# Spacing the loads, combinations and splits of the weight operands in the first layer of a two-layer encoder kernel

## The chip, the cores and the metric

The kernel runs on one core of a Trainium2 chip. The metric is the device time of one execution in microseconds (us). Three timed runs before the change took 2755.72, 2760.79 and 2751.14 us, so the median is 2755.72. A further execution was taken with the hardware profiler; all profile lines below are from it.

## The reference

Two layers over 2048 frames of width 1024, in float32. The change touches the first one, a chunked gMLP:

```
h = rms_norm(x, a_norm_g)
u, v, z = split(h @ w_in, 3)                  # w_in: 1024 x 6144
u = gelu(u);  v = layer_norm(gelu(v), ln_g, ln_b)
mixed = W_s(masked, per head) @ v in groups of 128 frames + b_s
x = x + (u * mixed * silu(z)) @ w_out         # w_out: 2048 x 1024
```

The second layer computes shared keys and values, a banded attention with a relative bias, a gate and an output product, and a last RMS norm ends the program. The second layer's code is not touched.

## The kernel before

**Numbers in two parts.** Each float32 operand of a product is split into a high part `hi` (an ACT cast to fp32r, L250) and a low part `lo` (source minus `hi`, on DVE, L253). `mm3` (L95) does hi x hi, hi x lo and lo x hi (L96, L97, L98), 128x128 against 128x512 each.

**Seven products for eight.** The input projection is made in six passes n = 0 to 5 (0 and 1 the two halves of v, 2 to 5 a quarter of u beside a quarter of z each), and the product with `w_out` in an output pass "o". Each multiplies a 2x2 block matrix by a 2x2 block matrix with seven block products, the phases 1 to 7, in the order `PH = (1, 2, 6, 5, 7, 4, 3)` (L439). The left operand of a phase is a block or a sum of blocks of the frames, `S`. The right one is a block or a combination of blocks of the weights, `T`. A phase has eight steps j, one for each pair of 128-frame blocks. A step of the input pass takes 4 x 3 matmuls into one PSUM tile `P`; passes 0 and 1 share their steps in phases 1 and 2, so those steps have twice as many. A step of the output pass takes 8 x 3 (tile `Po`). `evict` (L351) then brings the tile to SBUF: in phase 1 by an ACT copy (L357), else by a DVE sum with an earlier phase's tile (L353).

**Left operands.** In pass 0 they are made from normed frames by transposes and `s_split` (L390), and stored to memory (`hsd`, L397). Later passes load them with `s_load` (L383, DMA at L385) into six buffers `S`, asked for three steps ahead (`LOOK = 3`). In the output pass `prep_out` (L748) loads gated tiles (`A<-ytd`, four buffers), adds or subtracts them (phase 5 on DVE, L758; phase 7 on POOL, L762) and splits them (`So`).

**Right operands.** `make_t` (L258) has two functions for each piece q (two pieces in the input pass, four in the output one). `combine` loads 128x1024 pieces of weights, 512 KB each, into four buffers with the tag `raw` (L267; the profile's `rw`, `rwo`), and adds or subtracts them on POOL in halves of 512 columns (L272). Phase 6 takes three loads a piece and leaves a chain tile `ch` that phases 5 and 4 go on with; phase 7 takes two loads a piece, phases 1, 2, 3 and 4 one. `finish` splits the result into `T` (eight buffers; some phases use `hh` and `hl` instead).

**When things are listed.** `run_steps` (L442) goes from step -3 on. In each step it lists the events of the step, the product and eviction, the left operand of three steps later, and then what `add_t` (L458) has entered for that step. `add_t` computes `s = min(at + i, max(at, -1))`: where `at` is not negative, all pieces of a phase, loads, combinations and splits, come in the one step `at`, five steps before the phase starts. Phase 6 of passes 1 to 5 has its `combine` eight steps earlier still. The list is not yet the order on the engines. A planner goes through it with its own estimates of durations and may put an instruction whose inputs and buffers it holds ready earlier on its engine; each engine, and SP's queue that issues all DMAs, then runs its instructions strictly in the order so made. `behind` (L237) adds an edge for the planner between two instructions, with no semaphore; `in_order` uses it for the splits of left operands, and `merge_u` (L595) lists itself behind `last["evict"]`, the last DVE sum of an eviction.

**Around the products.** In passes 2 to 5, `uz_consts` (L543) loads `lg`, `lb` and the mixing weights `wr`, clears a corner on POOL (L554) and splits them to `ws`, all in one step, eight before the pass. `mix_prep` (L559) loads `va` (L564), applies the layer norm in two DVE instructions for each half (L568, L569) and splits to `vh`, `vl`, all in one step, four before the mixing products `mx` of `mix` (L577), which ACT evicts (L591). `done_uz` (L608) gates a finished tile through `later`, one to four steps after its eviction; `transposes` (L599) turns it on PE, ACT copies it out (L604) and it is stored to `ytd`. `flush` (L409) lists what has come due. After the last input step, `flush(1 << 30)` (L728) lists all that is left at once, ahead of the output pass. `block_norm` (L475) norms the frames at the start: ACT sums squares (L482), DVE adds EPS (L483), POOL takes the power (L484), DVE multiplies (L485).

Of the kernel before, what the change touches and what calls it, by code (L numbers as in the profile page):

```python
# [17 lines left out]
P = 128  # L18
# [15 lines left out]
def trunk_kernel(  # L34
# [174 lines left out]
    with ExitStack() as actx:  # L209
# [38 lines left out]

        def split(hi, lo, src, key=None):
            ins = nc.scalar.copy(hi, src)  # L250
            if key:
                in_order(key, ins)
            nc.vector.tensor_tensor(lo, src, hi.bitcast(F32), op=sub)  # L253
# [4 lines left out]
        def make_t(n, ph, src, nq, where, chain_of):  # L258
# [3 lines left out]
            vs = [None] * nq  # L262

            def combine(q):
                def raw(r, c):
                    t = sh.tile([P, 1024], F32, tag="raw", name=f"rw{n}_{ph}_{r}{c}{q}", bufs=4)
                    nc.sync.dma_start(t[:], src[r, c, q])  # L267
                    return t[:]

                def comb(o, x_, y_, op=sub):  # L270
                    for c in (slice(0, 512), slice(512, 1024)):
                        nc.gpsimd.tensor_tensor(o[:, c], x_[:, c], y_[:, c], op=op)  # L272
                    return o

                if ph in (1, 2, 3):
                    v = raw(*((0, 0), (1, 0), (1, 1))[ph - 1])
# [6 lines left out]
                elif n == "o":  # L283
                    if ph == 6:
                        if q == 0:
                            chain[n] = chain_of()
                        b = raw(1, 1)
                        v = comb(chain[n](q), b, raw(0, 1))
                        comb(v, v, raw(0, 0), add)
                    else:  # L290
                        v = raw(1, 1)
                        comb(v, v, chain[n](q))
                elif ph == 6:
                    if q == 0:
                        chain[n] = chain_of()
                    b = raw(0, 1)
                    t1 = comb(chain[n](2 + q), b, raw(0, 0))
                    v = comb(chain[n](q), raw(1, 1), t1)
                else:
                    v = chain[n](2 + q)  # L300
# [6 lines left out]
            return out, [  # L307
                [lambda q=q, f_=f_: f_(q) for q in range(nq)] for f_ in (combine, finish)
            ]

# [991 lines left out]
```

## Time and profile before

| | |
|---|---|
| median of 3 runs | 2755.72 us (2751.14 to 2760.79) |
| the profiled execution's own time | 2755.94 us |
| its span, first to last instruction | 2754.2 us |
| mean granted TensorE clock | 0.988 |
| input passes | to about 1086 us |
| output pass | about 1086 to 1425 us |
| DMA | 607.16 MB, mean 220 GB/s |
| PE idle before it, for S<-hsd | 15.6 us in 3 waits |

How to read the lines in the prediction. In a table of stretches, the columns are the stretch, its length, the busy time and number of instructions of PE, PEld (weight load), DVE, ACT and POOL, then the granted TensorE clock as a share of full speed, the DMA engines' mean busy share and GB/s. A timeline row has the start, the duration, the engine, the line, the operation, what it writes and reads, and in brackets the idle time of the engine before it and what ended that. SPq is the queue that issues the DMAs; the duration of a merged row there includes the waits between. A row of waits has the total us, the number and the longest. A row of a group has the busy time, the mean ns of one, and the idle time before them; a row of a tile or line gives min/median/max in ns and the first and last start in us. A DMA row has the size and the median us from issue to landing.

### The profile page before, as it was taken

How to read it: one execution, taken by the hardware profiler on the slowest of the kernel's cores; microseconds unless marked ns; L12 is line 12 of the kernel's file. 1: busy time of each engine (PE TensorE's matmuls, PEld its weight loads, DVE VectorE, ACT ScalarE, POOL GpSimd, SP SyncE). 2: the span in 40 equal slices, each digit the busy share in tenths (PEclk: the TensorE clock that was granted, in tenths of full speed). 3: DMA queues.
4: the chain of work that ended last, by engine and by line, in shares of the span. 5: the costliest groups of instructions: out<-in, count | busy, mean ns of one | idle time of the engine just before them, and what ended most of it. 6: DMA issues, size and time to landing. Idle time of an engine off the chain costs nothing.

```text
span 2754.2 us, 39945 instructions
## 1 busy us (share of the span) xinstructions
PE 2670.3 (97%) x14176; PEld 2269.1 (82%) x14176; DVE 1938.7 (70%) x3211; ACT 1274.9 (46%) x2244; POOL 717.1 (26%) x775
## 2 busy tenths in 40 slices
PE   8998989999999999998999999999999999999997
PEld 7787777888888877876888888899988999889996
DVE  5654556767567567676767676877778777887777
ACT  5422233443433424332235555566655666556663
POOL 4511124241231412536014531221112111121111
PEclk9999999999999999999999999999999999999998
DMA  8898997786877868767867665455554555453332
GB/s 288 318 322 295 334 341 281 262 309 231 312 266 241 307 204 287 278 228 252 295 198 235 223 196 190 154 153 154 157 167 159 154 152 151 145 169 112 121 111 69
DMA packets 209190, 607.16 MB, mean 220 GB/s; under 512 B 24288, under 2 KB 24288, under 8 KB 208992
## 3 DMA queue, kind: packets, MB, share of 16 engines
q1 hardware_dynamic: 208992, 604.62, 65.9%
q8 instruction: 113, 1.85, 0.3%
q14 instruction: 85, 0.70, 0.1%
HBM read 466.11 MB, written 127.93 MB: 216 GB/s over the span
## 4 chain that ended last, share of the span: by engine, by line
PE 44%; DVE 7%; DMA 5%; POOL 2%; issue 1%; ACT 1%; SPq 0%; DVEq 0%; POOLq 0%; ACTq 0%
PE pj L96 5%; PE pj L97 5%; PE pj L98 5%; PE s L973 4%; PE tp L1012 4%; PE pv L1039 4%; PE vp L96 2%; PE vp L98 2%; PE vp L97 2%; PE bo L96 2%; PE bo L97 2%; PE bo L98 2%; DMA rwo<-in_w_out 1%; DMA xr<-in_x 1%; DMA A<-ytd 1%
## 5 line engine op out<-in xcount | busy, mean ns | idle before, releaser
L96 PE MATMUL P<-T,S 128*128 128x512 f32 x1280 | 511.6, 400 | 18.2 <-DMA S<-hsd 15.6
L98 PE MATMUL P<-T,S 128*128 128x512 f32 x1280 | 504.0, 394 | 0.0
L97 PE MATMUL P<-T,S 128*128 128x512 f32 x1280 | 503.1, 393 | 0.5 <-DVE T L253 0.5
L992 POOL TENSOR_SCALAR pr<-pr,sl 128x640 f32<-128x640 f32 (+4 forms) x256 | 200.1, 782 | 759.5 <-DVE sl L991 669.7
L988 ACT ACTIVATE pr<-pr,nm 128x640 f32<-128x640 f32 (+4 forms) x256 | 195.5, 764 | 272.3 <-DVE nm L981 270.3
L96 PE MATMUL pj<-hh_b,wh_b 128*128 128x512 f32 x768 | 312.0, 406 | 0.7 <-ACT hh_b L150 0.7
L97 PE MATMUL pj<-hl_b,wh_b 128*128 128x512 f32 x768 | 302.7, 394 | 0.0
L98 PE MATMUL pj<-hh_b,wl_b 128*128 128x512 f32 x768 | 301.5, 393 | 0.0
L96 PEld LDWEIGHTS P<-T,S 128*128 128x128 f32 x1280 | 242.5, 189 | 63.7 <-DMA S<-hsd 14.0
L98 PEld LDWEIGHTS P<-T,S 128*128 128x128 f32 x1280 | 242.2, 189 | 51.7
L97 PEld LDWEIGHTS P<-T,S 128*128 128x128 f32 x1280 | 243.0, 190 | 44.9 <-DVE T L253 1.0
L1016 DVE TENSOR_TENSOR pt<-tp,pt 128x640 fp32r<-128x640 f32 (+4 forms) x256 | 188.6, 737 | 59.6 <-ACT pt L1015 57.0
L981 DVE CUSTOM_DVE_ANT_0 pr<-s,bias 128x640 f32<-128x640 f32 (+4 forms) x256 | 188.0, 735 | 44.5 <-PE s L973 41.1
L98 PEld LDWEIGHTS pj<-hh_b,wl_b 128*128 128x128 f32 x768 | 144.5, 188 | 33.3
L1015 ACT CAST pt<-tp 128x640 fp32r<-128x640 f32 (+4 forms) x256 | 159.3, 622 | 21.5 <-PE tp L1012 16.2
L1012 PE MATMUL tp<-ident,pr 128*128 128x128 f32 x1120 | 164.6, 272 | 4.4 <-DVE pt L1016 4.1
L96 PEld LDWEIGHTS pj<-hh_b,wh_b 128*128 128x128 f32 x768 | 144.9, 189 | 19.7 <-ACT hh_b L150 0.9
L1012 PEld LDWEIGHTS tp<-ident,pr 128*128 128x128 f32 x1120 | 134.4, 140 | 32.2 <-issue 5.9
L97 PEld LDWEIGHTS pj<-hl_b,wh_b 128*128 128x128 f32 x768 | 145.3, 189 | 17.4
L96 PE MATMUL vp<-wh_bv,hh_b 128*128 128x256 f32 x512 | 148.1, 289 | 1.5 <-ACT hh_b L150 0.9
L98 PE MATMUL vp<-wh_bv,hl_b 128*128 128x256 f32 x512 | 145.4, 284 | 0.6 <-DVE hl_b L151 0.4
L97 PE MATMUL vp<-wl_bv,hh_b 128*128 128x256 f32 x512 | 144.8, 283 | 0.0
(216 smaller groups left out, 6012.8 us busy)
## 6 DMA issues: line engine op xcount, KB each, us to landing
S<-hsd SPq DMA_DIRECT2D x288, 512.0 KB, 5.0
rw<-in_w_a SPq DMA_DIRECT2D x108, 512.0 KB, 5.8
raw_b<-wk SPq DMA_DIRECT2D x75, 512.0 KB, 4.0
A<-ytd SPq DMA_DIRECT2D x72, 512.0 KB, 5.1
hsd<-S SPq DMA_DIRECT2D x56, 512.0 KB, 3.8
rwo<-in_w_out SPq DMA_DIRECT2D x40, 512.0 KB, 5.0
bias<-reld SPq DMA_DIRECT2D x64, 320.0 KB, 3.7
raw_bo<-in_wb_out SPq DMA_DIRECT2D x36, 512.0 KB, 3.9
```

Source lines behind the costliest of these rows:

```text
L96: mm(ps, lh, rh, start=first, stop=False)
L97: mm(ps, lh, rl, start=False, stop=False)
L98: mm(ps, ll, rh, start=False, stop=last)
L973: mm(ps[:, sg, :w], q[:, qb * P : (qb + 1) * P], kx[:, koff + sg * w : koff + (sg + 1) * w], start=i == 0, stop=i == 1,)
L981: nc.vector.tensor_tensor_reduce(out=pr[:, c0:].rearrange("p (a b) -> p a b", a=nseg), in0=ps[:, :nseg, :w], in1=bias[:, c0:].rearrange("p ...
L988: nc.scalar.activation(pr[:, c0:], pr[:, c0:], AF.Exp, scale=-1.0, bias=nm[:], accum_out=sl[:])
L992: nc.gpsimd.tensor_scalar(pr[:, c0:], pr[:, c0:], sl[:], 1.0, op0=ALU.mult, op1=ALU.mult)
L1012: tpose(tp[:, b, :], pr[:, b * P : (b + 1) * P], ident[:])
L1015: nc.scalar.copy(oh, tp[:, b0:5, :])
L1016: nc.vector.tensor_tensor(pt[:, 1, b0 + qq : 5 + qq, cs], tp[:, b0:5, :], oh.bitcast(F32), op=ALU.subtract)
L1039: mm(po[:, 0, :], keys(i), pt[:, j, i, :], start=(t == 0 and j == 0 and i == blocks[0]), stop=(j == 1 and i == blocks[-1]),)
```

## The change

1. `make_t` has three functions now, `load`, `combine` and `finish`, and `add_t` enters each at its own offset from the phase's start, with a distance between the pieces: `(o, d)` puts piece q in step `start + o + d * q`.
2. `paced` puts an instruction behind `last["evict"]` in the planner's list. It is used for POOL's combinations, for the ACT half of splits that have no order of their own, for `lg`, `lb`, `wr`, `va` loads, the clearing of `wr`, and the first layer-norm instruction. The weight loads themselves aren't paced.
3. `uz_consts` is listed one step later, its clearing and split (`uz_ws`) four steps after it; the load of `va` (`mix_load`) two steps ahead of `mix_prep`.
4. The `flush(1 << 30)` goes. The output pass flushes step by step, and the pools are closed and opened in its step 4.
5. In phase 7 of the output pass one of the two subtractions goes from POOL to DVE. In `block_norm` the addition of EPS goes from DVE to POOL.

```diff
+        def paced(ins):
+            if "evict" in last:
+                behind(ins, last["evict"])
...
         def split(hi, lo, src, key=None):
             ins = nc.scalar.copy(hi, src)
             if key:
                 in_order(key, ins)
+            else:
+                paced(ins)
             nc.vector.tensor_tensor(lo, src, hi.bitcast(F32), op=sub)
...
+            rows = {}
+            need = {
+                1: [(0, 0)], 2: [(1, 0)], 3: [(1, 1)], 7: [(1, 1), (0, 1)], 4: [(1, 0)],
+                6: [(0, 1), (0, 0), (1, 1)], 5: [(1, 1)] if n == "o" else [],
+            }[ph]
+            def load(q):
+                for r, c in need:
+                    t = sh.tile([P, 1024], F32, tag="raw", name=f"rw{n}_{ph}_{r}{c}{q}", bufs=4)
+                    nc.sync.dma_start(t[:], src[r, c, q])
+                    rows[r, c, q] = t[:]
+            def comb(o, x_, y_, op=sub):
+                for c in (slice(0, 512), slice(512, 1024)):
+                    paced(nc.gpsimd.tensor_tensor(o[:, c], x_[:, c], y_[:, c], op=op))
+                return o
...
-        def add_t(ts, at, n, ph, src, nq, where, chain_of=None, ahead=0):
-            tops[n, ph], (cs, fs) = make_t(n, ph, src, nq, where, chain_of)
-            for i in range(nq):
-                s = min(at + i, max(at, -1))
-                ts.setdefault(max(s - ahead, -LOOK), []).append(cs[i])
-                ts.setdefault(s, []).append(fs[i])
+        def add_t(ts, at, n, ph, src, nq, where, chain_of, offs):
+            tops[n, ph], fs = make_t(n, ph, src, nq, where, chain_of)
+            for f_, (o, d) in zip(fs, offs):
+                for q in range(nq):
+                    s = at + o + d * q
+                    ts.setdefault(max(s, -LOOK), []).append(lambda f_=f_, q=q: f_(q))
...
-            nc.vector.tensor_scalar(r[:], r[:], EPS, None, op0=add)
+            nc.gpsimd.tensor_scalar(r[:], r[:], EPS, 1.0, op0=add, op1=mul)
...
+        def uz_ws(n):
+            wr = wsp[n]
+            paced(nc.gpsimd.memset(wr[64:128, :, 0:64], 0.0))
+            ws = up[0].tile([P, 2, 4, P], F32R, tag="ws", name=f"ws{n}", bufs=2)
             split(ws[:, 0], ws[:, 1], wr[:])
...
+        def mix_load(n, r, q):
+            va = mixp[n, r, q] = up[0].tile(
+                [P, 2, 512], F32, tag="va", name=f"va{n}_{r}_{q}", bufs=2
+            )
+            paced(nc.sync.dma_start(va[:], vd[n - 2, r, q][:]))
...
-                s = start[n, ph] - 5 if (n, ph) in start else start[0, ph] - 3
+                s = start.get((n, ph), start[0, ph])
+                if n == 0 or (n == 1 and ph in (1, 2)):
+                    offs = ((-6, 1), (-5, 1), (-4, 1))
+                elif ph == 6:
+                    offs = ((-13, 3), (-11, 3), (-5, 1))
+                elif ph == 4:
+                    offs = ((-14, 1), (-12, 1), (-5, 1))
+                else:
+                    offs = ((-8, 1), (-6, 1), (-5, 1))
                 if n == 1 and ph in (1, 2):
                     where = in_big(n, ph, ("hh",) if ph == 1 else ("hl",))
+                    offs = ((-5, 1), (-4, 1), (-3, 1))
...
-            at(b - 8, lambda n=n: uz_consts(n))
+            at(b - 7, lambda n=n: uz_consts(n))
+            at(b - 3, lambda n=n: uz_ws(n))
...
+                    at(b + o - 6, lambda n=n, r=r, q=q: mix_load(n, r, q))
                     at(b + o - 4, lambda n=n, r=r, q=q: mix_prep(n, r, q))
...
-        flush(1 << 30)
-        ux.close()
...
-                    for g in range(2):
-                        nc.gpsimd.tensor_tensor(v[:, g], v[:, g], b[:, g], op=sub)
+                    for g, eng in enumerate((nc.vector, nc.gpsimd)):
+                        eng.tensor_tensor(v[:, g], v[:, g], b[:, g], op=sub)
...
             def act_out(s, ph, j, views):
+                flush(nin + s)
...
+            at(4, poc_open)
...
-                add_t(ts, max(8 * i - 5, -LOOK), "o", ph, w_out, 4, where, cho)
+                offs = {6: ((-12, 2), (-11, 2), (-5, 1)), 4: ((-14, 1), (-13, 1), (-5, 1))}.get(
+                    ph, ((-7, 1), (-6, 1), (-5, 1))
+                )
+                add_t(ts, 8 * i, "o", ph, w_out, 4, where, cho, offs)
```

More of the change, by code (lines that the diff above doesn't have):

```diff
@@ L262, in make_t @@
             vs = [None] * nq
+            rows = {}
[12 more added lines that the diff above has]
+                return o
             def combine(q):
                 def raw(r, c):
[L266 to L273, printed above, removed]
+                    return rows.pop((r, c, q))
                 if ph in (1, 2, 3):
-                    v = raw(*((0, 0), (1, 0), (1, 1))[ph - 1])
+                    v = raw(*need[0])
                 elif ph == 7:
@@ L305, in finish @@
                 split(*out[q], vs[q])
-            return out, [
-                [lambda q=q, f_=f_: f_(q) for q in range(nq)] for f_ in (combine, finish)
-            ]
+            return out, (load, combine, finish)
         def in_t(n, ph):
@@ L561, in mix_prep @@
             lg, lb = lnw[n]
[L562 to L564 removed]
+            vf = mixp[n, r, q][:]
             for i in range(2):
@@ L596, in merge_u @@
             u = u0[n, j]
-            behind(nc.gpsimd.tensor_tensor(u, u, mt[n, 0, j // 2][:, j % 2, :], op=mul), last["evict"])
+            paced(nc.gpsimd.tensor_tensor(u, u, mt[n, 0, j // 2][:, j % 2, :], op=mul))
         def transposes(n, r, j, y):
@@ L727, in trunk_kernel @@
         run_steps(steps, ts, prep_in, act_in, events)
-        flush(1 << 30)
-        ux.close()
         po = pos[0]
-        with px, tc.tile_pool(name="poc", bufs=1, reuse_waits="tile") as poc:
+        pocs = []
+        with px:
             sc = {}
```

58 lines of the change are left out of this document (28 added, 30 removed).

## The prediction

> **What bounds the kernel now.** I read the page, then PE's busy time by stage and around its longest waits, then PE's timeline there, then the queues of what it had waited for.
>
> ```profile
> PE 2670.3 (97%) x14176; PEld 2269.1 (82%) x14176; DVE 1938.7 (70%) x3211; ACT 1274.9 (46%) x2244; POOL 717.1 (26%) x775
> ```
> ```profile
> 0.00:230.00 230.00, 209.85 (x1005) 172.00 (x1006) 138.26 (x188) 95.25 (x153) 86.90 (x80) 0.97 0.87 309
> 230.00:420.00 190.00, 179.18 (x788) 146.23 (x788) 105.35 (x154) 53.41 (x80) 26.05 (x20) 0.96 0.91 323
> 420.00:1086.00 666.00, 657.81 (x3126) 537.24 (x3125) 443.10 (x541) 256.54 (x413) 182.03 (x127) 0.99 0.79 272
> 1086.00:1425.00 339.00, 317.84 (x1392) 259.41 (x1392) 234.80 (x287) 103.69 (x158) 118.79 (x77) 0.98 0.71 244
> ```
> PE is busy for 97% of the span, so the change can only win what PE loses. It touches the first layer alone, to about 1425 us, where PE is idle for 20.2, 10.8, 8.2 and 21.2 us. The second cost of a wait is the clock behind it:
>
> ```profile
> 339.26 0.39 PE L97 MATMUL P<-T,S 128*128 128x512 f32 x1
> 339.49 0.39 PE L98 MATMUL P<-T,S 128*128 128x512 f32 x1
> 342.14 0.47 PE L96 MATMUL P<-T,S 128*128 128x512 f32 x1 [2.26 <-DMA S<-hsd]
> 345.00 0.63 PE L96 MATMUL P<-T,S 128*128 128x512 f32 x1
> 345.43 0.63 PE L97 MATMUL P<-T,S 128*128 128x512 f32 x1
> ```
> Before the wait, matmuls start 0.23 us apart, soon after it 0.43. Twelve at 0.227 make a step of the input pass, 2.72 us; a step of the output pass has 24, 5.45 us. I count a stretch's loss as its idle time plus its busy time times what its granted clock (behind POOL's count) lacks of 1.
>
> ```profile
> 210.00:240.00 30.00, 21.68 (x95) 17.18 (x94) 16.31 (x22) 10.68 (x16) 9.99 (x8) 0.83 0.74 252
> 335.00:350.00 15.00, 12.74 (x50) 10.06 (x49) 8.52 (x16) 4.42 (x6) 0.81 (x1) 0.89 1.03 375
> 385.00:405.00 20.00, 11.55 (x46) 8.95 (x45) 9.69 (x9) 6.95 (x10) 10.94 (x8) 0.74 0.80 302
> 460.00:480.00 20.00, 15.50 (x63) 11.96 (x63) 8.91 (x13) 4.42 (x8) 0.31 (x1) 0.83 0.88 310
> 1080.00:1100.00 20.00, 15.07 (x64) 11.32 (x63) 19.68 (x20) 9.43 (x16) 9.93 (x6) 0.83 0.72 239
> 1290.00:1310.00 20.00, 12.42 (x43) 8.93 (x43) 11.79 (x12) 5.32 (x8) 12.69 (x9) 0.83 0.71 242
> ```
> The losses are 8.3 + 3.7 = 12.0; 2.3 + 1.4 = 3.7; 8.5 + 3.0 = 11.5; 4.5 + 2.6 = 7.1; 4.9 + 2.6 = 7.5; 7.6 + 2.1 = 9.7. Together 51.5 us in 125 us of time. What stands behind the first and third is SP, which issues every DMA in the written-out order of one list:
>
> ```profile
> 204.89 12.25 SPq L267 DMA_DIRECT2D rw<-in_w_a  x6
> 217.66 0.42 SPq L385 DMA_DIRECT2D S<-hsd  x1
> ```
> ```profile
> 375.48 15.46 SPq L267 DMA_DIRECT2D rw<-in_w_a  x5
> 390.99 0.42 SPq L385 DMA_DIRECT2D S<-hsd  x1
> ```
> ```profile
> SPq L385 <- PE P L98: 324.4, 191, 9.1
> SPq L267 <- DVE T L253: 27.1, 15, 6.2
> ```
> ```profile
> S<-hsd SPq DMA_DIRECT2D x288, 512.0 KB, 5.0
> rw<-in_w_a SPq DMA_DIRECT2D x108, 512.0 KB, 5.8
> ```
> Weight loads (L267) held SP for 12.25 and 15.46 us, since a fifth needs one of four buffers back, which the DVE split (L253) frees. Only then came the left operand S. An S load waits for the product six before its own, so it has 5 x 2.72 = 13.6 us, of which landing takes 5.0. A hold of up to 8.6 us costs PE nothing; these two were longer. For the others:
>
> ```profile
> DVE va L568 <- DMA va<-vd: 49.0, 19, 9.5
> ```
> ```profile
> 470.77 0.62 ACT L250 CAST ws<-wr 128x512 fp32r<-128x512 f32 x1 [5.01 <-POOL wr L554]
> ```
> ```profile
> 1293.34 1.04 ACT L250 CAST To_hh<-cho 128x1024 fp32r<-128x1024 f32 x1 [5.83 <-POOL cho L272]
> ```
> ```profile
> PE mx L96 <- ACT m L591: 7.9, 6, 4.2
> PE ty L602 <- ACT yo L604: 4.8, 2, 3.2
> ```
> An instruction that uses a load was listed in the step of that load, so ACT (5.01, 5.83) and DVE (up to 9.5) stood in front of it with PE's next operand behind them.
>
> **The change, part by part.**
>
> *Spaced pieces.* Before, a phase loads, combines and splits its whole right operand in one step (phase 6 of pass 1 on combines eight steps ahead). Now loads come one to three steps before the combination, that one to eight steps before the split, pieces apart. In pass 2, phase 2 is loaded in steps 0 and 1 and split in 3 and 4; phase 6 is loaded in 3 and 6. The fifth load of 375.48 so meets a split due in its own step, not two loads and two splits. SP's hold falls from 15.46 us to about one load's landing and a split, 5.8 + 1.2 = 7.0, under 8.6. Of 11.5 I take back 10, and 10 of 12.0, where phase 3 and the next phase 6 were loaded in one heap. Nothing of the 3.7 at 335 us, where the DMA share is 1.03. The moved loads pass S loads and `vd` stores on SP and the moved combinations pass `merge_u` on POOL; none needs the other's data, and their count stays. Late next are S loads that the DMA engines themselves delay, as at 335 us.
>
> *Consumers behind loads.* The `ws` split comes four steps after its load, 10.9 us, against a wait of 5.01: I take 7 of 7.1. `mix_load` is two steps, 5.4 us, ahead of L568, and 512 KB land in 5 to 6 us; what that is worth is in the last term below. `lg` and `lb` move by one step and are needed eight steps later: nothing.
>
> *Output pass.* Four splits in one step are now four steps with one each; phase 4's loads precede its splits by nine. I take 8 of the 9.7 at 1290 and 4 of the other idle time of the pass (21.2 less 4.8 and 7.6). Half of phase 7's subtractions go from POOL to DVE:
>
> ```profile
> L762 POOL TENSOR_TENSOR A<-A,A 128x512 f32<-128x512 f32 x16 | 24.8, 1569 | 17.9 <-DMA A<-ytd 12.9 <-DVE xo L353 4.7
> L253 DVE TENSOR_TENSOR So<-A,So x64: 674/683/2383, 1128.3 to 1368.0; 128x512 fp32r<-128x512 f32 x64
> ```
> The eight on DVE cost 0.68 to 2.38 us each; I take 0.68, 5.5 us in a phase of 44 us, beside matmuls. DVE's long forms are those beside POOL's work. The Trainium skill, page "SBUF — State Buffer", section "Who interferes with whom", says that a DVE instruction with two SBUF inputs and a GpSimd one that reads SBUF exclude each other for a whole instruction. The 2383 ns beside 674 agree. By it the two halves come one after the other as before, and an estimate of 4 in place of 8 makes the result 2724.
>
> *Last gates.* The transposes of the last four steps (L602) ran in a row; now each stands between products of the output pass, and the 4.8 us of waits go. But the splits of the first output operand are now listed behind the last sum of the input pass:
>
> ```profile
> L250 ACT CAST T<-rw x44: 1031/1048/1060, 8.9 to 1036.1; 128x1024 fp32r<-128x1024 f32 x44
> L253 DVE TENSOR_TENSOR T<-rw,T x44: 1206/1218/2316, 11.5 to 1039.3; 128x1024 fp32r<-128x1024 f32 x44
> ```
> That costs from nothing, if they still run beside the last product, to 1.05 + 1.22 + 2.32 with the clock on top, 7. I take 4: of 7.5, 3.5 is left.
>
> *Ties.* Is a tie a wait? `merge_u` has one already:
>
> ```profile
> 599.87 6.41 POOL L597 TENSOR_TENSOR c<-c,m 128x512 f32<-128x512 f32 x4
> ```
> ```profile
> 612.11 0.68 DVE L353 TENSOR_TENSOR c<-P,x 128x512 f32<-128x512 f32 x1
> ```
> The first of these merges is tied to that sum and ran 12 us before it. So a tie sets places in the list, and holds no engine. Cost nothing; it keeps the list from filling idle places with prefetches. Weight loads themselves get no tie, and phase 1, whose eviction is an ACT copy, brings no new sum: there a tie reaches back to the pass before.
>
> *EPS on POOL.*
>
> ```profile
> L484 POOL TENSOR_TENSOR ra<-ra,mhalf 128x1 f32<-128x1 f32 x16 | 8.8, 551 | 33.7 <-DVE ra L483 33.7
> ```
> Sixteen small sums move in front of this power on POOL. Between a loss of 0.55 each, 8.8 us in all were they on the path, and an equal gain, since DVE need no longer stand still for ACT's sum of squares, I take a gain of 1. One more comes from PE's waits for `mx` beyond the 4.2 already counted (7.9 in all), by the earlier `mix_load`.
>
> The sum: 10 + 0 + 10 + 7 + 3.5 + 8 + 4 + 1 + 1 = 44.5. A newly listed order has new waits; I take off one as long as the longest here, 8.5. So 36 us are gained. The profiled execution took 2755.94, hardly off the median of 2755.72: **2720 us**.
>
> The clock can be weighed too:
>
> ```profile
> 1247.07 0.50 PE L98 MATMUL Po<-To_hh,So 128*128 128x512 f32 x1 [1.70 <-DVE So L253]
> 1247.41 0.39 PE L96 MATMUL Po<-To_hh,So 128*128 128x512 f32 x1
> ```
> A wait of 1.70 us left the pace alone (the next follows after 0.34 and then 0.23), one of 2.26 didn't. The Trainium skill, page "TensorE: Matmul & The Clock Gate", section "Why this matters for your kernels", puts the drop at gaps over about 3 us. The row of 2.26 disagrees; by the page, that wait would have cost no clock, and as I win nothing there, the sum stays; a remaining wait of 2 to 3 us would be cheaper by some 1.5.
>
> **The rivals.**
>
> *The DMA engines, not the list, set the early waits.*
>
> ```profile
> 360.00:380.00 20.00, 20.00 (x90) 16.58 (x89) 11.70 (x21) 6.73 (x11) 2.02 (x2) 1.00 1.02 394
> 380.00:400.00 20.00, 11.55 (x51) 8.88 (x50) 6.12 (x4) 6.44 (x11) 10.94 (x8) 0.78 0.70 263
> ```
> For it: a share of 1.02 and 394 GB/s just before; the same bytes must move. Against it: the share falls to 0.70 while PE waits, so there was room. Then the 20 us at 210 and 385 don't come: 44.5 - 20 - 8.5 = 16, **2740**.
>
> *Slower: buffers of weights crowd phases 7 and 4.* Phase 7 takes four loads in two steps and phase 4 now two more in the two after, through four buffers, and a combination on POOL must free the fifth. Where SP's hold there passes 8.6 us, S is late as at 375 us. One such place in each of passes 1 to 5, at 11.5 each, gives 57.5: 2755.9 - 44.5 + 57.5 = **2769**. For it: 15.46 us are on record from the same cause. Against it: two such instructions on POOL take 3.1 us (the mean of L762 twice), well under 8.6.
>
> *The list comes out much as before.* Ties hold nothing; the waits move, and the time stays at 2750 to 2763.
>
> **How the numbers follow.** Forecast 0.58, DMA 0.16, as before 0.09, crowding 0.17. The forecast's own range goes from 2700 (all of 51.5 and the 6 of small terms, no new wait: 2698) to 2746 (the tie at 7, POOL's 8.8 lost, and DVE's eight at 2.38: 36 - 3 - 9.8 - 13.6 = 9.6). The range for 8 in 10 takes in DMA, no change and nearly all of the crowding: 2699 to 2768. What a measurement here tells from no change is about 0.3%, 8.3 us: faster 0.74, within 0.09, slower 0.17.
>
> **What would show it.** Right: no SP row of L267 over 8.6 us; PE's wait for S<-hsd (15.6 now) under 5; L568's 49.0 halved; no transposes in a row at 1090; a wait of some us for `To` where the output pass starts; the subtraction on both engines. Wrong: waits for S where the DMA share is 1; rows of L267 as long as now near steps 24 to 28 of a pass; or splits (`T`) that PE waits for, because their loads are no longer early.

## The result: no change in time

The changed kernel takes 2756.2 us (median of 20 runs, 2751.4 to 2767.2), the kernel before 2756.7 beside it (20 runs). The ratio is 1.0003, with a 95% interval of 0.9993 to 1.0013. The forecast was 2720. The profiled execution of the changed kernel took 2751.53 us with a span of 2749.7 at a clock of 0.993; the profiled execution of a kernel lies up to some 8 us from the median of its runs here, so below sizes come from the timed ratios, and places from the profiles.

**The five stretches of the forecast again**, from the table of stretches of the changed kernel (columns as in the prediction):

```profile
210.00:240.00 30.00, 28.41 (x137) 23.36 (x136) 18.34 (x26) 10.03 (x17) 10.41 (x8) 1.00 0.97 349
385.00:405.00 20.00, 18.72 (x89) 15.45 (x88) 8.93 (x9) 6.01 (x11) 14.41 (x10) 1.00 0.97 354
460.00:480.00 20.00, 20.00 (x97) 16.03 (x96) 11.39 (x13) 7.05 (x12) 8.75 (x5) 1.00 0.88 311
1080.00:1100.00 20.00, 13.49 (x48) 10.15 (x47) 19.12 (x20) 10.41 (x16) 7.13 (x4) 0.74 0.74 256
1290.00:1310.00 20.00, 14.54 (x50) 11.12 (x50) 13.59 (x18) 4.45 (x7) 7.86 (x5) 0.83 0.89 297
```
By the prediction's own measure (idle time, and busy time times what the clock lacks of 1) the losses are now 1.6; 1.3; 0.0; 6.5 + 3.5 = 10.0; 5.5 + 2.5 = 8.0. Before they were 12.0, 11.5, 7.1, 7.5 and 9.7. The three terms of the input passes came: 27.7 us, where 27 were forecast. The two of the output pass didn't: 2.5 lost and 1.7 won, where 3.5 and 8 were to be won.

The DMA queue of the changed kernel shows why the first three came. Here is its timeline where the row of 15.46 us stood:

```profile
374.30 5.70 SPq L279 DMA_DIRECT2D rw<-in_w_a  x3
380.09 1.34 SPq L396 DMA_DIRECT2D S<-hsd  x3
383.12 5.66 SPq L279 DMA_DIRECT2D rw<-in_w_a  x3
389.35 1.44 SPq L396 DMA_DIRECT2D S<-hsd  x3
```
The forecast said about 7.0 for a hold; they are 5.70 and 5.66, with S loads between them, and PE no longer starves there. What PE, and DVE's layer norm, wait for in the changed kernel (us in total, times, longest):

```profile
PE mx L96 <- ACT m L612: 10.6, 9, 1.7
PE Po L96 <- ACT So L255: 7.9, 3, 5.6
PE t L405 <- DVE hb L496: 7.7, 3, 3.4
PE Po L97 <- DVE To L260: 5.6, 2, 3.1
PE P L96 <- DMA S<-hsd: 5.6, 4, 2.3
PE Po L96 <- ACT To L255: 3.4, 1, 3.4
```
```profile
DVE va L588 <- DMA va<-vd: 0.2, 1, 0.2
```
`S<-hsd` fell from 15.6 to 5.6 (under 5 was named as the sign), and DVE's wait for `va` from 49.0 to 0.2. But `hb` (the norm of the first frames), `To` and `mx` are new or longer.

**Where the 27.7 us went.** Four rows of each kernel cut the first layer into stretches: the first and the last sum `c<-P,x`, the first copy `xo<-Po`, and the last sum `yo<-Po,yo`. Before the change:

```profile
L353 DVE TENSOR_TENSOR c<-P,x x48: 670/682/692, 74.2 to 963.8; 128x512 f32<-128x512 f32 x48
...
L357 ACT COPY xo<-Po x8: 577/589/591, 1100.9 to 1144.4; 128x512 f32<-128x512 f32 x8
...
L353 DVE TENSOR_TENSOR yo<-Po,yo x8: 671/680/692, 1382.2 to 1423.6; 128x512 f32<-128x512 f32 x8
```
The same rows of the changed kernel (the two times behind the durations are the first and the last start):

```profile
L364 DVE TENSOR_TENSOR c<-P,x x48: 667/685/692, 82.7 to 955.4; 128x512 f32<-128x512 f32 x48
...
L368 ACT COPY xo<-Po x8: 577/587/590, 1098.6 to 1139.6; 128x512 f32<-128x512 f32 x8
...
L364 DVE TENSOR_TENSOR yo<-Po,yo x8: 676/691/692, 1377.8 to 1419.4; 128x512 f32<-128x512 f32 x8
```
The table takes these rows from the profile of every kernel of this study. "To first c" is the start, "to last c" most of the input passes, "to first xo" the turn to the output pass, "to last yo" the output pass; what is left of the span is 1328 to 1334 us in all of them. The ratio of each kernel is to runs of the kernel before taken beside it; kernels of different rows are compared by ratio. The input passes of p1, c1, q3 and q4 are written the same, and their profiles spread over 2 us to the first `c` and 6 us from there to the last, so a smaller difference between two profiles isn't told apart from scatter. The kernels are told in the next section.

| kernel | ratio to before [95%] | to first c | to last c | to first xo | to last yo |
|---|---|---|---|---|---|
| before | 1 | 74.2 | 889.6 | 137.1 | 322.7 |
| changed | 1.0003 [0.9993, 1.0013] | 82.7 | 872.7 | 143.2 | 320.8 |
| e1 first weights as before | 0.9996 [0.9981, 1.0011] | 78.2 | 876.2 | 146.9 | 319.7 |
| e2 EPS on DVE | 1.0002 [0.9988, 1.0017] | 79.4 | 870.4 | 144.8 | 323.2 |
| e3 first To splits not tied | 0.9993 [0.998, 1.0006] | 82.7 | 870.9 | 138.4 | 324.1 |
| e4 weight loads tied too | 1.011 [1.0089, 1.0131] | 82.8 | 891.2 | 146.7 | 331.0 |
| p1 spaced passes 1, 2 alone | 0.9931 [0.9912, 0.995] | 76.3 | 860.4 | 138.7 | 322.7 |
| t0 changed, no ties | 0.9988 [0.9974, 1.0003] | 82.4 | 862.4 | 136.7 | 334.1 |
| o1 output part alone | 1.0027 [1.0011, 1.0043] | 77.5 | 884.2 | 134.6 | 332.8 |
| c1 p1 and o1 | 0.9964 [0.995, 0.9979] | 77.4 | 865.6 | 136.6 | 331.1 |
| q1 p1, ties in input | 0.9984 [0.9971, 0.9997] | 76.9 | 873.1 | 143.1 | 324.7 |
| q2 p1, new start | 0.9945 [0.993, 0.996] | 82.5 | 865.8 | 137.5 | 323.6 |
| q3 p1, last gates inside | 0.9917 [0.9899, 0.9934] | 76.7 | 866.3 | 135.2 | 326.1 |
| q4 c1, ties in output | 0.99 [0.9883, 0.9917] | 75.5 | 862.7 | 134.7 | 324.4 |
| s1 changed less three steps | 0.9928 [0.9913, 0.9942] | 78.7 | 863.7 | 135.7 | 320.4 |
| s2 changed, no ties in input | 0.9947 [0.9934, 0.996] | 81.5 | 864.1 | 141.5 | 317.4 |
| s3 q1, combinations not tied | 0.9999 [0.9987, 1.0011] | 77.6 | 878.8 | 142.0 | 329.2 |
| s4 p1, combinations tied | 0.9949 [0.9933, 0.9964] | 76.2 | 870.3 | 140.7 | 323.8 |
| r1 q1, layer norm not tied | 0.9974 [0.9962, 0.9986] | 77.6 | 873.5 | 138.6 | 330.3 |
| r2 p1, layer norm tied | 0.9984 [0.9968, 1.0] | 76.7 | 875.9 | 137.6 | 320.8 |

The changed kernel loses 8.5 us at the start, wins 16.9 in the input passes (where kernels with spaced pieces and no ties in the input passes win 23 to 29), loses 6.1 at the turn, and wins 1.9 in the output pass.

### The profile page after: what moved, and what is told of

Its sections match the earlier page's. It is cut to its first block, busy times and chain, and to the rows that moved or that the text cites. A ratio compares the mean times of both kernels' runs of the same rounds, so it can differ in the third digit from the quotient of the medians.

```text
span 2749.7 us, 39875 instructions
## 1 busy us (share of the span) xinstructions
PE 2668.6 (97%) x14176; PEld 2266.3 (82%) x14176; DVE 1942.4 (71%) x3203; ACT 1271.3 (46%) x2244; POOL 733.7 (27%) x783
## 5 line engine op out<-in xcount | busy, mean ns | idle before, releaser
L364 DVE TENSOR_TENSOR x<-P,x 128x512 f32<-128x512 f32 x144 | 98.8, 686 | 76.5 <-PE P L98 76.5
```

The source lines that it names most:

```text
L364: last["evict"] = nc.vector.tensor_tensor(*args, **kw).ins.name
```

## Experiments: what each part costs

My theory after the result: the spaced pieces win what was forecast, and three things that I had priced at nothing or as a gain eat it: the new start, the ties, and the output pass. The rival: the list as a whole came out no better, and whatever one stretch wins another loses.

**One step of the change undone at a time.** The weights of phase 1 of passes 0 and 1 go back to step -3 (e1):

```diff
                     offs = ((-5, 1), (-4, 1), (-3, 1))
+                if ph == 1 and n < 2:
+                    offs = ((-3, 1), (-3, 1), (-3, 1))
```


> The changed kernel with one thing undone: the pieces of phase 1 of passes 0 and 1 are listed in steps -3 and -2 as before, not all loads in step -3. Theory A (the changed kernel loses about 9 us at the start, because four weight loads of 512 KB now stand in SP's queue ahead of the third frame block): the first DVE sum of an eviction (c<-P,x) comes at 74 to 76 us instead of 82.7, and the time falls by 6 to 9 us. Theory B (it is the addition of EPS on POOL, which makes frames wait for POOL): the sum stays near 82.7 us and the time is that of the changed kernel.

EPS goes back to DVE (e2):

```diff
-            nc.gpsimd.tensor_scalar(r[:], r[:], EPS, 1.0, op0=add, op1=mul)
+            nc.vector.tensor_scalar(r[:], r[:], EPS, None, op0=add)
```


> The changed kernel with the addition of EPS back on DVE, nothing else. Theory A (weight loads ahead of the frames): the first DVE sum stays at 82 to 84 us and the time does not move by over 3 us. Theory B (EPS on POOL): the sum comes back to 74 to 76 us and the time falls by 6 to 9 us.

Both show in the place, neither in the time: the first `c` starts at 78.2 and 79.4 instead of 82.7, and the ratios stay at 0.9996 and 1.0002. The DMA queue at the start, before the change and after it, shows the first of the two:

```profile
2.10 0.92 SPq L267 DMA_DIRECT2D rw<-in_w_a  x2
3.06 1.01 SPq L477 DMA_DIRECT2D ha<-in_x  x2
```
```profile
2.10 1.97 SPq L279 DMA_DIRECT2D rw<-in_w_a  x4
4.11 0.51 SPq L488 DMA_DIRECT2D ha<-in_x  x1
12.97 0.33 SPq L408 DMA_DIRECT2D hsd<-S  x1
13.34 0.43 SPq L488 DMA_DIRECT2D ha<-in_x  x1
```
Four weight loads are issued ahead of the third block of frames now, not two, and the fourth block is asked for at 13.34 us, where it had been asked for by 4.07. The two effects don't add: s1 below, which undoes both (and the ties of the input passes), has its first `c` at 78.7, no earlier than e1 alone. The kernels with the whole start of before lie between 74.2 and 77.6.

The splits of the first output operand lose their tie (e3), and weight loads get one (e4):

```diff
-            else:
+            elif tied:
                 paced(ins)
...
-                split(*out[q], vs[q])
+                split(*out[q], vs[q], tied=(n, ph) != ("o", 1))
```


> The changed kernel, but the splits of the right operand of the output pass's first phase are not tied behind the last sum of the input pass. Theory A (the tie puts these splits behind that sum, and PE waits 3.4 and 3.1 us for To at the start of the output pass, with the clock some 10 us in all): both waits for To go, PE's idle time from 1080 to 1100 us falls from 6.5 to under 2, and the time falls by 4 to 8 us. Rival (ACT and DVE are full there with the last gates, whatever the tie): the waits stay within 2 us of their sum, under another name.

```diff
-                    nc.sync.dma_start(t[:], src[r, c, q])
+                    paced(nc.sync.dma_start(t[:], src[r, c, q]))
```


> The changed kernel with the weight loads tied behind the last sum as well. Theory A (loads without a tie are listed some ten steps early, so phase 7's combinations run on POOL beside the splits and layer norms of DVE at step 22 of passes 3 to 5, and PE waits 1.7 us for mx there): PE's waits for mx (10.6 us in 9) fall under 5 us and the time by 2 to 6 us. Rival (the mx waits come from where the split of phase 5 and the layer norm are listed, whatever POOL does): they stay at 8 us or more.

Without its tie the turn to the output pass takes 138.4 us and not 143.2; the time, 0.9993, isn't told apart from 1.0003. The two waits that this takes away stand in the changed kernel's PE timeline:

```profile
1085.07 1.61 PE L96 MATMUL Po<-To,So 128*128 128x512 f32 x3 [3.43 <-ACT To L255]
1090.62 0.80 PE L97 MATMUL Po<-To,So 128*128 128x512 f32 x1 [3.08 <-DVE To L260]
```
More ties, on the other hand, cost: 1.1%, nearly 19 us of it against the changed kernel between the first and the last `c`, and PE's waits for `mx` didn't fall (11.6 us in 8).

**The parts alone.** p1 has the spaced pieces in pass 1 (from phase 6 on) and pass 2 only, the `ws` split apart from its loads, the early `va` load in pass 2, no ties, and everything else as before the change; an offset that is a single number stands for the old listing:

```diff
         def paced(ins):
-            if "evict" in last:
-                behind(ins, last["evict"])
+            return
...
+                if n not in (1, 2) or (n == 1 and ph < 3):
+                    s = max(s - (5 if (n, ph) in start else 3), -LOOK)
+                    offs = 8 if n and ph == 6 else 0
```


> The kernel before with one part of the change alone: spaced weight pieces in passes 1 (from phase 6 on) and 2, the mixing weights' load and split apart, and the earlier load of va in pass 2. No ties, start, passes 3 to 5 and output pass as before. Theory A (the change takes away the long holds of SP, and other parts of it give the time back): the waits of 4.9, 8.5 and 4.2 us at 226, 398 and 472 us go, nothing new comes, and the time falls by 18 to 28 us against the kernel before. Rival (what is won by 480 us is lost again later whatever is listed there, since some other work falls behind): PE is 12 us or more ahead at the end of pass 2, but the time falls by under 8 us.

The changed kernel with no tie but `merge_u`'s own (t0) has only the first of these two edits:

> The changed kernel without the ties, all spacing kept (merge_u keeps its own). Theory A (the ties cost only where the output pass begins, and hold back nothing else): 3 to 8 us faster than the changed kernel, by the two waits for To at 1085 and 1091 us. Rival (the ties are what keeps prefetches from crowding the queues): waits for S come back and it is over 8 us slower than the changed kernel.

The output part alone (o1) has the changed output pass, untied, and the input passes of before; c1 is p1 with that output pass:

```diff
+                if True:
+                    s = max(s - (5 if (n, ph) in start else 3), -LOOK)
+                    offs = 8 if n and ph == 6 else 0
```


> The kernel before with the part of the output pass alone: the spaced pieces there, the last gates listed within it, half of phase 7's subtraction on DVE, no ties, the input passes as before. Theory A (the output part in itself is worth about what was forecast, and the tie and a crowded DVE took it back): 8 to 16 us faster than before. Rival (in the output pass the waits move from phase 7 to phase 6's splits, and the part is worth nothing): within 5 us of before, with PE waits for To near the start of phase 6.

> The two parts of the last kernels but one together: spaced pieces in passes 1 and 2 and in the output pass, no ties, start and passes 3 to 5 as before. Theory A: the gains add, 25 to 40 us faster than before. Rival (what is won early is lost later): under 10 us.

p1 takes 2734.9 us, 0.9931: a small part of the change wins 19 us and keeps them to the end, so nothing takes a won us back later by itself. The rival falls. o1 loses, 1.0027, and c1 is behind p1, with intervals that touch. The place is one wait in the output pass. From c1, the DMA queue and PE:

```profile
1199.02 13.34 SPq L278 DMA_DIRECT2D rwo<-in_w_out  x4
1218.12 0.33 SPq L161 DMA_DIRECT2D raw_b<-in_w_kqz  x1
...
1224.08 0.42 SPq L776 DMA_DIRECT2D A<-ytd  x1
```
```profile
1230.97 0.79 PE L98 MATMUL Po<-To_hh,So 128*128 128x512 f32 x1 [9.61 <-DVE So L259]
```
Weight loads hold the queue for 13.34 us, with the second layer's loads behind them, and the left operand `A` is asked for only at 1224.08. It is the mechanism of my second rival, crowded buffers of weights, in another pass than I looked for it, but the hold alone doesn't do it: p1, whose output pass is listed as before the change, has a row of 17.00 us with five of these loads at 1183.77, `A` follows at once at 1200.87, and PE has no such wait. In c1 the second layer's loads stand between.

**p1 with one piece added** (q1 to q4). q1 adds the ties of the input passes, q2 the new start with EPS on POOL, q3 the last gates within the output pass; q4 is c1 with ties in the output pass alone, except for phase 1. The edit of q1, with the ties off from the output pass on:

```diff
+        tie = [1]
         def paced(ins):
-            return
+            if tie and "evict" in last:
+                behind(ins, last["evict"])
...
         run_steps(steps, ts, prep_in, act_in, events)
+        tie.clear()
```


> The kernel with spaced pieces in passes 1 and 2 alone (ratio 0.9931 to before, about 2737 us against 2756) gets the ties back in all six input passes; its output pass stays untied. Theory A, the ties themselves cost passes 3 to 5 what the changed kernel loses there against its version without ties (lead at the last eviction of pass 5: 6.0 us with ties, 18.1 without): this kernel is 6 to 12 us slower than the one without ties, so 2743 to 2749 us, ratio 0.995 to 0.9975, and PE waits again for mx in passes 3 to 5. Rival B, the ties cost only where the weights of passes 3 to 5 are spaced too (they are not here): within 3 us of 2737. Rival C, ties help the list: faster than 2734.

```diff
-                if n not in (1, 2) or (n == 1 and ph < 3):
+                if n not in (0, 1, 2):
...
-            nc.vector.tensor_scalar(r[:], r[:], EPS, None, op0=add)
+            nc.gpsimd.tensor_scalar(r[:], r[:], EPS, 1.0, op0=add, op1=mul)
```


> The kernel with spaced pieces in passes 1 and 2 alone gets the new start: the weights of pass 0 and of phases 1 and 2 of pass 1 at the changed offsets, and the addition of EPS on POOL. Theory A, what the start loses (8.6 us at the sixteenth eviction in the changed kernel) is not recovered later: 6 to 10 us slower than 2737, so 2743 to 2747 us, and the first sum of an eviction starts near 82 us instead of 76. Rival B, later waits absorb it, since loads that had delayed PE then arrive in time: within 3 us of 2737.

```diff
-        flush(1 << 30)
...
             def act_out(s, ph, j, views):
+                flush(nin + s)
...
-            poc_open()
+            at(4, poc_open)
```


> The kernel with spaced pieces in passes 1 and 2 alone lists its last gates and transposes step by step within the output pass; the output pass's weights and the subtraction of phase 7 stay as before. Theory A, the transposes between products take away the waits at the start of the output pass (4.8 us idle and the clock behind them in 1080 to 1100 us of the kernel before) and cost nothing in its place: 3 to 7 us faster than 2737, so 2730 to 2734 us. Rival B, with the gates listed later the last tiles come later too, and loads of gated tiles or the first To splits stand behind them: within 2 us of 2737 or slower, with new waits between 1085 and 1130 us.

```diff
+        tie = []
...
         run_steps(steps, ts, prep_in, act_in, events)
+        tie.append(1)
```


> Spaced pieces in passes 1 and 2 without ties, and the output part as in the change, with its ties except for the splits of phase 1. The same without ties took 2743.74 us (ratio 0.9964), with a wait of PE of about 10 us near 1235 to 1248 us, where weight loads stand in front of loads of gated tiles. Theory A, ties in the output pass hold the combinations back and spread the loads, so that one wait goes: 2735 to 2739 us, the output pass costs no more than before, and no wait of PE is over 6 us there. Rival B, the ties only move the wait to another place, as in the changed kernel (waits of 2.6 us at 1187 and 5.6 at 1294): 2741 to 2746 us.

q1: the ties cost 0.9984 - 0.9931, 15 us, more than I expected. q2: the new start costs 6.2 us to the first `c` in the profile; its ratio, 0.9945, is worse than p1's by 4 us, with intervals that overlap. q3: the turn is 3.5 us shorter, the time not told apart from p1. q4 is the fastest of the study: 2729.6 us, 0.99 [0.9883, 0.9917], ahead of the kernels before and after. In its DMA queue the loads of `A` come between those of the weights:

```profile
1187.53 5.77 SPq L281 DMA_DIRECT2D rwo<-in_w_out  x2
1196.92 0.33 SPq L780 DMA_DIRECT2D A<-ytd  x1
...
1201.52 1.53 SPq L780 DMA_DIRECT2D A<-ytd  x2
```
```profile
PE Po L96 <- ACT So L257: 7.4, 2, 5.5
```
So ties pay in the output pass, and cost in the input passes. The size of the gain is less sure: from c1 to q4 it is 0.0064 in the time, over 17 us, but the profiles show only 6.7 in the output pass (331.1 to 324.4); from t0 to the changed kernel they show 13.3 there. That is why the changed kernel without any tie is hardly better: t0 wins 10.3 us to the last `c` and 6.5 at the turn, and gives back 13.3 in the output pass.

**Do the costs add up, and which tie is it?** s1 is the changed kernel less three steps (no ties in the input passes, phase 1 of the output pass not tied, the old start); s2 only leaves out the ties of the input passes. Both use the edits above.

> The whole change less three of its steps: no ties in the input passes, the splits of the output pass's phase 1 not tied, and the start as before (the weights of phase 1 of passes 0 and 1 listed in step -3, EPS on DVE). Theory A, these three are what gives the gain back: the spaced pieces of passes 3 to 5 and the earlier loads are then worth nothing either way, and the time is that of the kernel with both parts and ties in the output pass alone (2729.6 us, ratio 0.99): 2726 to 2736. Rival B, another part that is in the change and not in that kernel costs too (spaced weights in passes 0 and 3 to 5): 2739 us or more.

> The change without its ties in the six input passes; the output pass keeps them, and the start is the changed one. Theory A, ties cost in the input passes 10 to 14 us and pay in the output pass: 2740 to 2747 us (2756 less that, and 1 to 2 left for the tied first splits). Rival B, ties in both passes hang together, and the output pass loses again what the input passes win, as in the changed kernel without any tie (2751): 2748 us or more.

s2 comes out at 0.9947: the ties of the input passes cost the changed kernel 0.0056, 15 us. s1 comes out at 0.9928, between the two theories and 20 us ahead of the changed kernel. Read as a ladder, the ratios are p1 0.9931, q4 0.9900, s1 0.9928, s2 0.9947, changed 1.0003: -19 us for pieces in passes 1 and 2, -9 for the output part with ties, +8 for the pieces of the other passes and the earlier `va` loads there, +5 for the start and the first splits, +15 for the ties of the input passes. The three middle steps have intervals that overlap a little; the first and the last stand clear. The +8 has no place in the profiles: those of q4 and s1 have spans of 2730.4 and 2730.3 us. Of the +15, they show 8.6 us up to the last `c` (872.7 to 864.1).

s3 takes q1 and leaves the combinations untied; s4 ties only them; r1 takes q1 and leaves the `va` load and the layer norm untied; r2 ties only those:

```diff
-                    paced(nc.gpsimd.tensor_tensor(o[:, c], x_[:, c], y_[:, c], op=op))
+                    nc.gpsimd.tensor_tensor(o[:, c], x_[:, c], y_[:, c], op=op)
```


> The kernel with spaced pieces in passes 1 and 2 alone and ties in the input passes (2751.8 us, ratio 0.9984), with the ties of POOL's combinations taken away. Theory A, a tied combination of phase 7 runs later than it could, beside DVE's layer norm, and makes that take 1.4 to 1.8 us for each instruction instead of 0.75: without those ties the layer norm has 0.75 again, PE's waits for mx of 0.96 and 1.36 us go in passes 3 to 5, and 6 us or more come back: 2740 to 2746. Rival B, another tied instruction (the layer norm itself, the split, the load of va) has been moved beside the combination: still 2749 to 2753, with the long layer norm instructions.

> The kernel with spaced pieces in passes 1 and 2 alone, with ties of POOL's combinations in the input passes and of nothing else. Theory A (the combinations are what costs): 2745 to 2752 us, with layer norm instructions of 1.4 to 1.8 us. Rival B (another tied instruction costs): 2734 to 2740, as without any tie.

```diff
-            paced(nc.sync.dma_start(va[:], vd[n - 2, r, q][:]))
+            nc.sync.dma_start(va[:], vd[n - 2, r, q][:])
...
-                paced(
-                    nc.vector.scalar_tensor_tensor(o, o, lmv[:, r, j, 0:1], lg[:], op0=sub, op1=mul)
-                )
+                nc.vector.scalar_tensor_tensor(o, o, lmv[:, r, j, 0:1], lg[:], op0=sub, op1=mul)
```


> The kernel with spaced pieces in passes 1 and 2 alone and ties in its input passes (2751.8 us, ratio 0.9984), without the ties of the load of va and of the layer norm. Theory A, these two ties bring the layer norm so close to its mixing products that POOL's or DVE's other work makes it late: the last layer norm starts again some 22 us ahead of the last mixing product, the waits for mx of about 1 and 1.4 us in passes 3 to 5 go, and the time is 2738 to 2745 us. Rival B, the short lead is only a mark of the tied list and something else costs: 2748 us or more, though the lead is back.

> The kernel with spaced pieces in passes 1 and 2 alone, with the ties of the load of va and of the layer norm and no other. Theory A: 2746 to 2756 us, a lead of the last layer norm of 9 to 15 us, and waits for mx in passes 3 to 5. Rival B: 2734 to 2742 us, whatever the lead.

The ties of the `va` load and the layer norm alone cost 0.0053 against p1, as much as all ties (r2). But taking them away brings back only 0.0010, not told apart from nothing (r1), and the combinations' ties alone lengthen the input passes by 4 to 10 us in the profile against the kernels without ties there, though in the time s4 isn't clear of p1. No one tie is the cause: with spaced pieces, the stretch to the last `c` takes 860 to 866 us in every kernel without ties there and 870 to 891 in every kernel with any set of them, and the sets don't add. For s3 and r1 my theory A was wrong, and s3's 2756 us lie above its rival's range too; s4 fell between its two.

What a tie does can be read from r2 near 580 us, where the fourth layer norm of pass 3 stands: the load of its `va` on SP, then DVE, POOL and PE.

```profile
575.34 0.38 SPq L591 DMA_DIRECT2D va<-vd  x1
```
```profile
580.87 2.48 DVE L601 SCALAR_TENSOR_TENSOR va<-va,lmv,lg 128x512 f32<-128x512 f32 x2 [0.78 <-DMA va<-vd]
583.27 3.49 DVE L603 SCALAR_TENSOR_TENSOR va<-va,lrs,lb 128x512 f32<-128x512 f32 x2
...
587.93 2.32 DVE L265 TENSOR_TENSOR vl<-va,vh 128x1024 fp32r<-128x1024 f32 x1 [0.56 <-ACT vh L260]
```
```profile
577.32 5.49 POOL L289 TENSOR_TENSOR ch<-rw,ch 128x512 f32<-128x512 f32 x4 [2.43 <-DMA rw<-in_w_a]
582.76 10.87 POOL L631 TENSOR_TENSOR c<-c,m 128x512 f32<-128x512 f32 x6
```
```profile
590.30 0.39 PE L97 MATMUL mx<-vl,ws 128*128 128x256 f32 x1 [1.78 <-DVE vl L265]
```
and the same layer norm in p1: the load, the first and the last of its four instructions, its split, and its first product.

```profile
555.68 0.33 SPq L585 DMA_DIRECT2D va<-vd  x1
```
```profile
559.78 0.74 DVE L595 SCALAR_TENSOR_TENSOR va<-va,lmv,lg 128x512 f32<-128x512 f32 x1
...
563.62 0.75 DVE L597 SCALAR_TENSOR_TENSOR va<-va,lrs,lb 128x512 f32<-128x512 f32 x1
...
581.53 1.22 DVE L259 TENSOR_TENSOR vl<-va,vh 128x1024 fp32r<-128x1024 f32 x1
```
```profile
586.87 0.28 PE L96 MATMUL mx<-vh,ws 128*128 128x256 f32 x1
```
`va` has two buffers. p1 asks for this one as soon as the split that read the buffer last is done, at 555.7 us; in r2 that split is done at 557.5, and the load is asked for 18 us later. So r2's layer norm starts 7.4 us ahead of its first product (588.24), p1's 27.1, with POOL idle beside it (558.30 to 564.02). In r2 it falls beside work of POOL: two instructions of 0.75 take 3.49, the split 2.32 for 1.22, and PE waits 1.78. p1's next layer norm, at 575.61, is lengthened beside POOL too (1.21, 1.19 and 1.77 us for 0.75), and it costs nothing, since its product comes at 602.36. In passes 3 to 5 the layer norm starts at least 19 us ahead of its product in the kernel before, p1 and t0, but only 10.9 us in the changed kernel, 6.5 in r2 and 5.5 in q1, at the least. The lost lead isn't the whole cost: in r1 it is back (15 us or more), PE's waits for `mx` between 480 us and the last `c` fall to 0.7 us, but waits of 5.2 us for `ty` come in their place, and the time hardly moves.

In the changed kernel a split `T` stands between the first two instructions of such a layer norm and is lengthened, beside a combination:

```profile
616.00 2.31 DVE L260 TENSOR_TENSOR T<-ch,T 128x1024 fp32r<-128x1024 f32 x1
618.23 0.74 DVE L590 SCALAR_TENSOR_TENSOR va<-va,lrs,lb 128x512 f32<-128x512 f32 x1
```
```profile
611.01 6.21 POOL L284 TENSOR_TENSOR rw<-rw,rw 128x512 f32<-128x512 f32 x3
```
```profile
622.44 0.39 PE L96 MATMUL mx<-vh,ws 128*128 128x256 f32 x1 [1.73 <-ACT m L612]
```
ACT idles 2.88 us until that layer norm is done, splits it, and only then makes the eviction `m`, which PE waits for. In s3, without the tied combinations, the layer norm was mostly short again and yet late: DVE waits 47.2 us for `va`. The wait of 1.73 comes once in each of passes 2 to 5 (1.73 or 1.74 us each time). Between 480 us and the last `c`, PE waits 5.8 us for `mx` and 2.9 for `ty` in the changed kernel and 1.3 in all in t0; that is most of the 10.3 us between these two profiles. No run isolates the share of any one wait, and what the other ties do in detail stays open.

## Why the prediction was wrong, point by point

- *Spaced pieces, 10 + 0 + 10, and consumers behind loads, 7.* Right: 10.4, 10.2 and 7.1 came, by the mechanism named (holds of 5.70 and 5.66 us where 7.0 was forecast). p1 keeps 19 us of it. The two rows of 12.25 and 15.46 us were read from stretches that begin inside them: in full they are 13.26 and 18.28 us, with eight loads each, which changes neither argument nor sum.
- *Ties: "Cost nothing."* This is the step that failed most. A tie isn't a wait, that was right, but it isn't free: it moves an instruction in a list that every engine obeys, and what then stands beside it or behind it pays. Measured: 15 us lost by the ties of the input passes (s2 against the changed kernel). What is seen there is loads and layer norms that come later, with a lead of at least 10.9 us over their product where it had been at least 19; which tie costs how much stays open. In the output pass ties are a gain (c1 to q4, 0.0064 with intervals apart), which I had mentioned in half a sentence and not priced.
- *Last gates, 3.5 of 7.5.* The tie of the first splits costs 4.8 us in the profile (143.2 to 138.4), near the 4 taken. The gain of 7.5 didn't come: even without the tie the turn takes 138.4, against 137.1 before. On top of p1 it is 3.5 (q3), and hardly to be seen in the time.
- *Output pass, 8 and 4.* Failed: 1.9 us won with ties, 8 to 11 lost without them (o1, c1, t0). I priced the splits one by one and didn't follow the weight loads through the four buffers past the loads of `A`, although my second rival had part of the rule: I placed it in passes 1 to 5, where no such hold appeared. DVE's half of the subtraction is a small part of this: 0.94 us (the median of eight) where 0.68 was taken.
- *EPS on POOL, a gain of 1.* No gain is seen: undoing it (e2) brings the first `c` 3.3 us earlier. And the new offsets of the first weights were not priced at all: undoing those of phase 1 (e1) brings 4.5 us. The two don't add (78.7 in s1), so only the loss of the whole start is clear of scatter (82.7 against 74.2 to 77.6). I had written that SP issues every DMA in the written-out order, and didn't look at the first 14 us of that queue. In time, both together cost about 4 (q2), not apart from nothing.
- *Waits for `mx`, 1.* DVE's wait for `va` went as foreseen, and PE's wait for `mx` rose from 7.9 to 10.6 all the same. Before, the layer norm ran at least 19 us ahead of its product in passes 3 to 5, so DVE's 49.0 us cost PE little; in the change the lead is shorter, and in the place shown above a lengthened split uses it up.
- *One new wait, 8.5.* Too small: what came in was the start, the turn and the ties. My third rival, that the list comes out as before, had the time, but not the cause: its premise that ties hold nothing fell with s2, and 27.7 us of waits went by the mechanism that I had named and were lost again elsewhere. That 2756 lies in the range of 2699 to 2768 is no merit of the sum: the range took in "no change", which had a chance of 0.09.

## What to carry to other kernels

Price an edge that only orders a list like any move: follow what it displaces, engine by engine, and ask which engine then runs beside which. Split a change by stage before judging it: here a part worth 1% and a part costing 1% gave no change, and undoing small steps in the whole told nothing about time until the large cost was out. In any queue that runs in order, go through its first 15 us and through each place where loads with few buffers stand ahead of loads that the next product needs.

## What the hardware showed

DVE and POOL lengthen each other: a layer norm instruction of 0.74 us takes 1.75 beside POOL's work (3.49 for two, r2), and POOL's `c<-c,m` takes 1.81 there (10.87 for six) where two take 2.56 in p1 (at 582.72). The Trainium skill, page "SBUF — State Buffer", section "Who interferes with whom", says that a DVE instruction with two SBUF inputs contends with a GpSimd one that reads SBUF; the rows of r2 and p1 agree. What a tied list costs so hangs on what stands beside the instruction that makes PE's next operand, and on how far ahead of PE that runs.

The granted clock doesn't follow the length of a wait alone. In r2, a wait of 2.10 us leaves the matmuls behind it 0.23 us apart; one of 2.34 at the same place of the next pass drops them to 0.43, from 1.2 us after it, for 3.4 us:

```profile
555.68 0.39 PE L96 MATMUL mx<-vh,ws 128*128 128x256 f32 x1 [2.10 <-ACT m L625]
...
557.06 0.39 PE L97 MATMUL P<-T,S 128*128 128x512 f32 x1
557.29 0.40 PE L98 MATMUL P<-T,S 128*128 128x512 f32 x1
```
```profile
735.18 0.39 PE L96 MATMUL mx<-vh,ws 128*128 128x256 f32 x1 [2.34 <-ACT m L625]
...
737.17 0.63 PE L98 MATMUL P<-T,S 128*128 128x512 f32 x1
737.59 0.63 PE L96 MATMUL P<-T,S 128*128 128x512 f32 x1
```

A wait of 1.96 us at 771.68 in the same kernel, with one of 0.42 at 773.31 behind it, drops the pace as well, to 0.43 from 774.08 on, though it is shorter than the 2.10 that didn't.
